# FFN-down: a seven-product square at every second visit in three of the four sweeps

## The chip, the cores and the metric

The kernel runs on one core of one Trainium2 chip. The metric is the device time of one execution in microseconds. Three runs of the kernel before took 1183.07, 1184.19 and 1185.29 us; the median, 1184.19 us, is its time. The engines are named as in the profile: PE multiplies matrices (PEld loads its stationary operand), DVE and ACT work on vectors, POOL is the general engine, and SP issues nearly all loads.

## The reference

One layer of a decoder trunk over 256 tokens with a residual stream of 2048 columns, in float32. After a mixer (pooling and RWKV-7 heads), it computes

```python
h2 = rms_norm(x, mlp_norm[i])
x = x + jnp.square(jax.nn.relu(h2 @ w_ffn_up[i])) @ w_ffn_down[i]
gate = jax.nn.sigmoid(rms_norm(x, ple_norm[i]) @ w_ple_gate[i])
x = x + gate * (p[i] @ w_ple_proj[i])
return rms_norm(x, final_norm)
```

The second line is the FFN: up from 2048 to 8192 columns (FFN-up), a squared ReLU, and down from 8192 to 2048 (FFN-down). The change is in FFN-down.

## The kernel before

**Precision.** Every float32 operand is split into a high half, a copy rounded by ACT to the matmul's format, and a low half, the difference, which DVE computes. A product of two matrices is three matmuls: high times high, high times low, low times high.

**Stages.** A head, the RWKV and pooling work with its input projections, the output projection, and then two halves of the FFN (`ffn_half`, L1301). Each half has FFN-up, which makes eight activation tiles `y` (128 x 2048, high and low half), and two sweeps of FFN-down (`down_sweep`, L1206), one for each 1024 output columns (`pair` 0 and 1). So FFN-down has four sweeps: first half pair 0, first half pair 1, second half pair 0, second half pair 1. After them come the projection of the per-layer embeddings, the gate and the final norm.

**One sweep.** A sweep has 16 visits, one for each `kp`. A visit takes a square of 2 x 2 blocks of the activation (two blocks of 128 features, two of 128 tokens) and two rows of weights of 1024 columns, `rx` and `ry`, each loaded by one DMA of 512 KB on SP (`load_raw`, L149). An ordinary visit (L1277 to L1282) splits both rows (`halves_of`: two ACT copies of 512 columns and one DVE subtraction of 1024 for each row) and does eight block products, 24 matmuls of 512 columns. A seven-product square (L1257 to L1275) is a Strassen-Winograd step: it forms four sums of weight blocks on DVE (`t1` to `t4`, L1268 to L1271, 512 columns each), splits seven weight blocks (one of 512 columns, `wad` in the profile, and three of 1024) and does seven block products, 21 matmuls. In the profile the weights of visit n are named `d_na` and `d_nb` in an ordinary visit; `d_nb`, `d_nc`, `d_nd` and `wad` in a square. The products gather in eight PSUM banks, of which four (`b1`, `b5`, `b6`, `b7`) belong to the squares alone and are added to the result after the last square (L1283 to L1294); the other four are added at the sweep's end (L1297). After the last square of the fourth sweep the transposition of the normalised stream for the gate begins (`between`, `h3t` in the profile).

**Sums of activations.** A square also needs four sums of its activation blocks, high and low half. `activation_sums` (L1191) makes them during FFN-up, as soon as the tile's square is there, for each `kp` in `SEVEN`. Two sets share one tile, and the tiles are taken from slots 0, 2 and 5 of the activation pool. Both sweeps of the half read them.

**Which visits.** `SEVEN` is (1, 3, 6, 8, 11, 13). The first three sweeps use all six, the fourth uses (1, 3, 6, 11): 22 squares in 64 visits. Pair 0 goes through `kp` in order; pair 1 goes 0, 2, 1, 4, 3, 5, 6, ... 15. A place below is the position in that order, counted from 0.

**Order and buffers.** From the end of the output projection on, a scheduler sets the order of instructions on each engine from the program order and priorities: weight splits have priority 20000, the last additions 30000. Six buffers hold raw weights (three `raw`, three `raw2`). High halves have three buffers, low halves three, both shared by all visits; in a square, `wad`, the four weight sums (slot 1) and the fourth split (`graw`, two buffers) have their own. In the fourth sweep hooks at places 5, 8, 11 and 14 (`keep`, L1167) each load and split one part of the last gate panel; its raw load also takes a `graw` buffer. The loads on SP start in the order in which they are issued.

Of the kernel before, what the change touches and what calls it, by code (L numbers as in the profile page):

```python
# [10 lines left out]
F32R = mybir.dt.float32r  # L11
# [29 lines left out]
def trunk(  # L41
# [107 lines left out]
    def load_raw(src, n, name):  # L149
        own = False  # L150
        if deep:
            deep.append(name)
            own = len(deep) > 5 and len(deep) % 6 < 3
        if own:
            raw = fp.tile([128, 1024], F32, tag="raw2", bufs=3, name=f"raw_{name}")
        else:
            raw = wp.tile([128, 1024], F32, tag="raw", name=f"raw_{name}")
        nc.sync.dma_start(raw[:, 0:n], src)
        return raw
# [11 lines left out]
    def split_sb(h_ap, l_ap, src_ap):  # L171
        nc.scalar.activation(h_ap, src_ap, AF.Copy)
        nc.vector.tensor_tensor(l_ap, src_ap, h_ap.bitcast(F32), op=ALU.subtract)
# [115 lines left out]
    def a8(slot, name, dt=F32):  # L289
        return act.tile([128, 2048], dt, tag=f"a{slot}", name=name)  # L290
# [801 lines left out]
    fp = ctx.enter_context(tc.tile_pool(name="fp", bufs=1))  # L1092
# [92 lines left out]

    SEVEN = (1, 3, 6, 8, 11, 13)
    s_slots = (0, 2, 5)

    def activation_sums(box, kp, r):  # L1191

        i = SEVEN.index(kp)
        if i % 2 == 0:
            box[kp] = box[SEVEN[min(i + 1, len(SEVEN) - 1)]] = a8(s_slots[i // 2], f"S{kp}", F32R)
        st = box[kp][:, i % 2 * 1024 : i % 2 * 1024 + 1024]
        t_ = fp.tile([128, 1024], F32, tag="junk", bufs=1, name=f"s{kp}")
        s1, s2_, s3, s4 = (t_[:, j * 128 : (j + 1) * 128] for j in range(4))
        a11, a21, a12, a22 = (r[:, j * 128 : (j + 1) * 128] for j in range(4))
        nc.vector.tensor_tensor(s1, a21, a22, op=ALU.add)  # L1200
        nc.vector.tensor_tensor(s3, a11, a21, op=ALU.subtract)
        nc.vector.tensor_tensor(s2_, s1, a11, op=ALU.subtract)
        nc.vector.tensor_tensor(s4, a12, s2_, op=ALU.subtract)
        split_sb(st[:, 0:512], st[:, 512:1024], t_[:, 0:512])

    def down_sweep(hf, pair, ys, sboxes, hooks=(), between=None, seven=SEVEN):  # L1206

# [16 lines left out]
        def prod(n, a_, w_):  # L1224
            first, last = left[n] == todo[n], left[n] == 1
            left[n] -= 1
            (ah, al), (wh, wl) = a_, w_
            nc.tensor.matmul(banks[n], ah, wh, start=first, stop=False)  # L1228
            nc.tensor.matmul(banks[n], ah, wl, start=False, stop=False)  # L1229
            nc.tensor.matmul(banks[n], al, wh, start=False, stop=last)  # L1230

        def halves_of(src, name, own=False):

            pool, kw = (fp, dict(bufs=2)) if own else (wp, {})
            wh = pool.tile([128, 1024], F32R, tag="graw" if own else "wh", name=f"wh_{name}", **kw)
            wl = pool.tile([128, 1024], F32R, tag="graw" if own else "wl", name=f"wl_{name}", **kw)
            with tc.high_priority(20000):
                for c in range(2):
                    nc.scalar.activation(wh[:, c * 512 : c * 512 + 512], src[:, c * 512 : c * 512 + 512], AF.Copy)
                nc.vector.tensor_tensor(wl, src, wh.bitcast(F32), op=ALU.subtract)  # L1240
            return [(wh[:, c * 512 : c * 512 + 512], wl[:, c * 512 : c * 512 + 512]) for c in range(2)]
# [5 lines left out]
        def add(tt, c, src):  # L1247
            nc.vector.scalar_tensor_tensor(xs(tt, c), src, s2[:, tt : tt + 1], xs(tt, c), op0=ALU.mult, op1=ALU.add)

        for q, kp in enumerate((0, 2, 1, 4, 3, *range(5, 16)) if pair else range(16)):  # L1250
            if q in hooks:
                hooks[q]()
            y, j = ys[kp // 2], kp % 2 * 512
            a11, a21, a12, a22 = ((y[:, j + i * 128 : j + i * 128 + 128], y[:, 1024 + j + i * 128 : 1152 + j + i * 128]) for i in range(4))
            rx, ry = (load_raw(w_down[pair, hf * 32 + 2 * kp + i], 1024, f"{nm}_{kp}_{i}") for i in range(2))
            if kp in seven:
                i = SEVEN.index(kp)  # L1257
                st = sboxes[kp][:, i % 2 * 1024 : i % 2 * 1024 + 1024]
                s1, s2_, s3, s4 = ((st[:, c * 128 : c * 128 + 128], st[:, 512 + c * 128 : 640 + c * 128]) for c in range(4))
                t_ = a8(1, f"t{nm}_{kp}")  # L1260
                t1, t3, t2, t4 = (t_[:, c * 512 : c * 512 + 512] for c in range(4))
                wa = fp.tile([128, 1024], F32R, tag="wa", name=f"wa{nm}_{kp}")
                w11 = wa[:, 0:512], wa[:, 512:1024]
                with tc.high_priority(20000):
                    split_sb(*w11, rx[:, 0:512])
                w21, w22 = halves_of(ry, f"{nm}_{kp}b")
                with tc.high_priority(20000):
                    nc.vector.tensor_tensor(t1, rx[:, 512:1024], rx[:, 0:512], op=ALU.subtract)  # L1268
                    nc.vector.tensor_tensor(t3, ry[:, 512:1024], rx[:, 512:1024], op=ALU.subtract)
                    nc.vector.tensor_tensor(t2, t3, rx[:, 0:512], op=ALU.add)  # L1270
                    nc.vector.tensor_tensor(t4, ry[:, 0:512], t2, op=ALU.subtract)  # L1271
                w1, w3 = halves_of(t_[:, 0:1024], f"{nm}_{kp}c")
                w2, w4 = halves_of(t_[:, 1024:2048], f"{nm}_{kp}d", True)
                for n, a_, w_ in (("1", a11, w11), ("2", a12, w21), ("3", s4, w22), ("5", s1, w1), ("7", s3, w3), ("6", s2_, w2), ("4", a22, w4)):
                    prod(n, a_, w_)  # L1275
            else:
                w11, w12 = halves_of(rx, f"{nm}_{kp}a")  # L1277
                for n, a_, w_ in (("2", a11, w11), ("4", a21, w11), ("3", a11, w12), ("x", a21, w12)):
                    prod(n, a_, w_)
                w21, w22 = halves_of(ry, f"{nm}_{kp}b")  # L1280
                for n, a_, w_ in (("2", a12, w21), ("4", a22, w21), ("3", a12, w22), ("x", a22, w22)):
                    prod(n, a_, w_)  # L1282
            if kp == seven[-1]:  # L1283
                u = fp.tile([128, 512], F32, tag="r", bufs=2, name=f"u{nm}")
                with tc.high_priority(20000):
                    add(0, 0, b1)
                    nc.scalar.activation(u, b1, AF.Copy)
                    nc.vector.tensor_tensor(u, b6, u, op=ALU.add)
                    add(0, 1, b5)
                    add(1, 1, b5)  # L1290
                    add(0, 1, u)
                    nc.vector.tensor_tensor(u, b7, u, op=ALU.add)
                add(1, 0, u)
                add(1, 1, u)  # L1294
                if between is not None:
                    between()
# [4 lines left out]
    def ffn_half(hf):  # L1301
        sboxes = {}
        ys = []
        for i in range(8):
            f = hf * 8 + i
            y = fp.tile([128, 2048], F32R, tag="y", bufs=8, name=f"y{f}")

            def square(bi, bank):
                r = fp.tile([128, 512], F32, tag="r", bufs=2, name=f"r{f}_{bi}")
                r2 = r.rearrange("p (c t) -> p c t", c=2)  # L1310
                nc.scalar.activation(r2, bank[:, :, T : 2 * T], AF.Copy)
                nc.vector.tensor_tensor(r2, bank[:, :, 0:T], r2, op=ALU.add)
                nc.vector.scalar_tensor_tensor(r, r, 0.0, r, op0=ALU.max, op1=ALU.mult)
                split_sb(y[:, bi * 512 : bi * 512 + 512], y[:, 1024 + bi * 512 : 1024 + bi * 512 + 512], r)
                if 2 * i + bi in SEVEN:
                    activation_sums(sboxes, 2 * i + bi, r)

            gemm_wide(w_up[f], h2, f"u{f}", square)
            ys.append(y)
            if f == 1:  # L1320
                inv_ms()

        if hf == 1:
            h3_part, h3 = transposed("h3")
            h3_box.append(h3)

        down_sweep(hf, 0, ys, sboxes)
        if hf == 0:
            down_sweep(hf, 1, ys, sboxes)
        else:  # L1330
            down_sweep(hf, 1, ys, sboxes, {5: keep, 8: keep, 11: keep, 14: keep}, lambda: [h3_part("ple_norm", n) for n in range(2)], (1, 3, 6, 11))
            for n in range(2, 4):
                h3_part("ple_norm", n)

# [149 lines left out]
```

## Time and profile before

| | |
|---|---|
| median of three runs | 1184.19 us |
| the profiled execution | 1184.84 us |
| its span, first to last instruction | 1183.1 us |
| mean granted TensorE clock | 0.997 |
| FFN-down, first half (two sweeps) | 558.9 to 725.0 us of the span |
| FFN-down, second half | 903.3 to about 1073 us of the span |
| PE, DVE, ACT busy | 1166.3, 857.5, 704.5 us |

A row of the timeline gives the start in us from the span's start, the duration, the engine (with a q for its sequencer, which issues DMAs), the line of the kernel, the operation, what is written and read, shapes and a count; in brackets stands the idle time of the engine before it and what ended it. PE's matmuls overlap in these rows, so their rate is read from start to start. A row of windows gives a stretch, its length, and for each engine the busy time in it. A row of one tile gives the least, median and largest duration in ns.

### The profile page before, as it was taken

What the parts mean: (1) busy time and instruction counts of PE and PEld (TensorE: products, weight loads), DVE (VectorE), ACT (ScalarE), POOL (GpSimd) and SP (SyncE); (2) the same over time, 40 slices, a digit from 0 to 9 for tenths busy, and PEclk for the clock granted to TensorE, in tenths of its full rate; (3) what the DMA queues carried; (4) which work ended last, traced back from release to release, by engine and by line L of the source; (5) the groups of instructions that cost most, each with busy time, mean ns of one, the idle gap of its engine ahead of it and who ended that gap; (6) DMA issues with size and microseconds to landing.
All of it is one profiled execution on the core that took longest, in us unless ns stands there. A gap on an engine that the chain in (4) does not pass through costs nothing.

```text
span 1183.1 us, 17263 instructions
## 1 busy us (share of the span) xinstructions
PE 1166.3 (99%) x6428; PEld 976.6 (83%) x6428; DVE 857.5 (72%) x1156; ACT 704.5 (60%) x1302; POOL 13.6 (1%) x73
## 2 busy tenths in 40 slices
PE   9999999999999999999999999999999999999997
PEld 8787777888887888888888888888888888878886
DVE  7686995964656666667888977666678779788543
ACT  7776848676545465555565654554556555668544
POOL 2100000000000000000000000000000000000000
PEclk9999999999999999999999999999999999999999
DMA  8464443354455555656556665655555556767611
GB/s 290 151 198 148 130 144 122 119 179 157 163 199 177 178 181 194 193 184 209 196 183 209 210 217 178 193 185 193 188 188 205 203 195 207 275 219 252 197 54 71
DMA packets 60756, 216.81 MB, mean 183 GB/s; under 512 B 6784, under 2 KB 7552, under 8 KB 60288
## 3 DMA queue, kind: packets, MB, share of 16 engines
q1 hardware_dynamic: 60240, 215.12, 54.5%
q8 instruction: 50, 0.82, 0.3%
q10 hardware_dynamic: 432, 0.60, 0.1%
q14 instruction: 34, 0.28, 0.1%
HBM read 213.59 MB, written 2.10 MB: 182 GB/s over the span
## 4 chain that ended last, share of the span: by engine, by line
PE 95%; ACT 2%; DVE 1%; DMA 1%; issue 0%; POOL 0%; SPq 0%; ACTq 0%; POOLq 0%
PE u_w L1112 20%; PE u_w L1117 10%; PE d_b L1229 8%; PE d_b L1230 8%; PE d_b L1228 8%; PE gt_b L238 2%; PE gt_b L242 2%; PE gt_b L241 2%; PE d_w L1229 2%; PE d_w L1230 2%; PE d_w L1228 2%; PE zk_b L241 1%; PE zk_b L242 1%; PE o_b L241 1%; PE o_b L242 1%; PE zv_b L238 1%
## 5 line engine op out<-in xcount | busy, mean ns | idle before, releaser
L1112 PE MATMUL u_w<-h,wh_u 128*128 128x512 f32 x1024 | 322.2, 396 | 0.0
L167 ACT ACTIVATE wh_u<-raw_u 128x512 fp32r<-128x512 f32 x256 | 147.6, 624 | 163.1 <-issue 96.1
L168 DVE TENSOR_TENSOR wl_u<-raw_u,wh_u 128x1024 fp32r<-128x1024 f32 x128 | 156.7, 1225 | 110.9 <-ACT wh_u L167 109.0
L1117 PEld LDWEIGHTS u_w<-h,wl_u 128*128 128x128 f32 x1024 | 192.5, 188 | 45.1
L1117 PE MATMUL u_w<-h,wl_u 128*128 128x256 f32 x1024 | 201.5, 278 | 0.0
L1112 PEld LDWEIGHTS u_w<-h,wh_u 128*128 128x128 f32 x1024 | 156.0, 189 | 0.1
L168 DVE TENSOR_TENSOR wl_gt<-raw_gt,wh_gt 128x1024 fp32r<-128x1024 f32 x24 | 29.4, 1224 | 23.2 <-ACT wh_gt L167 23.1
L167 ACT ACTIVATE wh_gt<-raw_gt 128x512 fp32r<-128x512 f32 x48 | 28.0, 639 | 23.1 <-PE gt_b L242 14.4
L241 PE MATMUL gt_b<-wh_gt,h 128*128 128x512 f32 x96 | 37.4, 389 | 0.0
L242 PE MATMUL gt_b<-wh_gt,h 128*128 128x512 f32 x96 | 37.4, 389 | 0.0
L168 DVE TENSOR_TENSOR wl_o<-raw_o,wh_o 128x1024 fp32r<-128x1024 f32 x16 | 19.6, 1223 | 12.9 <-ACT wh_o L167 9.9
L167 ACT ACTIVATE wh_o<-raw_o 128x512 fp32r<-128x512 f32 x32 | 18.4, 623 | 16.2 <-issue 8.4
L167 ACT ACTIVATE wh_zp<-raw_zp 128x512 fp32r<-128x512 f32 x32 | 18.6, 623 | 15.9 <-PE zp_b L242 5.7
L168 DVE TENSOR_TENSOR wl_zk<-raw_zk,wh_zk 128x1024 fp32r<-128x1024 f32 x16 | 19.5, 1222 | 9.4 <-ACT wh_zk L167 9.3
L241 PE MATMUL zv_b<-wh_zv,hTh 128*128 128x512 f32 x64 | 26.0, 407 | 0.0
L241 PE MATMUL zk_b<-wh_zk,hTh 128*128 128x512 f32 x64 | 25.8, 404 | 0.0
L241 PE MATMUL zp_b<-wh_zp,hTh 128*128 128x512 f32 x64 | 25.7, 402 | 0.0
L238 PE MATMUL gt_b<-wl_gt,h 128*128 128x512 f32 x96 | 25.7, 389 | 0.0
L242 PE MATMUL zk_b<-wh_zk,hTl 128*128 128x512 f32 x64 | 25.6, 401 | 0.0
L241 PE MATMUL zr_b<-wh_zr,hTh 128*128 128x512 f32 x64 | 25.5, 398 | 0.0
L168 DVE TENSOR_TENSOR wl_zv<-raw_zv,wh_zv 128x1024 fp32r<-128x1024 f32 x16 | 19.4, 1219 | 8.2 <-ACT wh_zv L167 7.3
L242 PE MATMUL zp_b<-wh_zp,hTl 128*128 128x512 f32 x64 | 25.0, 391 | 0.0
(809 smaller groups left out, 2941.4 us busy)
## 6 DMA issues: line engine op xcount, KB each, us to landing
raw_u<-in_w_ffn_up_dram SPq DMA_DIRECT2D x128, 512.0 KB, 3.5
raw_d<-in_w_ffn_down_dram SPq DMA_DIRECT2D x128, 512.0 KB, 4.3
raw_gt<-in_w_ple_gate_dram SPq DMA_DIRECT2D x24, 512.0 KB, 3.4
raw_zk<-in_w_in_dram SPq DMA_DIRECT2D x16, 512.0 KB, 3.6
raw_zr<-in_w_in_dram SPq DMA_DIRECT2D x16, 512.0 KB, 3.4
raw_zv<-in_w_in_dram SPq DMA_DIRECT2D x16, 512.0 KB, 3.4
raw_zp<-in_w_in_dram SPq DMA_DIRECT2D x16, 512.0 KB, 3.3
raw_o<-in_w_out_dram SPq DMA_DIRECT2D x16, 512.0 KB, 4.1
```

The lines of the kernel that those rows point to most:

```text
L167: nc.scalar.activation(wh[:, a * 512 : (a + 1) * 512], raw[:, a * 512 : (a + 1) * 512], AF.Copy)
L168: nc.vector.tensor_tensor(wl, raw, wh.bitcast(F32), op=ALU.subtract)
L238: nc.tensor.matmul(banks[tt], ah[:, ts_], halves[a][1], start=False, stop=last)
L241: nc.tensor.matmul(banks[tt], ah[:, ts_], halves[a][0], start=i + a == 0, stop=False)
L242: nc.tensor.matmul(banks[tt], al[:, ts_], halves[a][0], start=False, stop=False)
L1112: nc.tensor.matmul(bank[:, ct, :].rearrange("p (s t) -> p s t", s=2), wh[:, cs[ct]], hl, start=k == 0, stop=False, skip_group_check=True,)
L1117: nc.tensor.matmul(bank[:, ct, 0:T], wl[:, cs[ct]], hl[:, 0, :], start=False, stop=k == 15, skip_group_check=True)
L1228: nc.tensor.matmul(banks[n], ah, wh, start=first, stop=False)
L1229: nc.tensor.matmul(banks[n], ah, wl, start=False, stop=False)
L1230: nc.tensor.matmul(banks[n], al, wh, start=False, stop=last)
```

## The change

`SEVEN` gets seven members, all odd: (1, 3, 5, 7, 9, 11, 13). A square stands at every second visit. The first three sweeps use all seven, so each has nine ordinary visits instead of ten. The set of sums for 13 has no partner and gets a tile of its own in another pool (`S`, 1024 columns). In pair 1 of the first half the order becomes 0, 2, 1, 4, 3, 6, 5, 8, 7, 10, 9, 12, 11, 14, 13, 15, which puts the squares at places 2, 4, 6, 8, 10, 12, 14; pair 1 of the second half keeps its order. There the fourth sweep uses (1, 3, 7, 11) instead of (1, 3, 6, 11), since 6 no longer has sums. In all there are 25 squares in 64 visits.

```diff
-    SEVEN = (1, 3, 6, 8, 11, 13)
+    SEVEN = (1, 3, 5, 7, 9, 11, 13)
     s_slots = (0, 2, 5)
...
         if i % 2 == 0:
-            box[kp] = box[SEVEN[min(i + 1, len(SEVEN) - 1)]] = a8(s_slots[i // 2], f"S{kp}", F32R)
+            st = a8(s_slots[i // 2], f"S{kp}", F32R) if i < 6 else fp.tile([128, 1024], F32R, tag="S", name=f"S{kp}")
+            box[kp] = box[SEVEN[min(i + 1, len(SEVEN) - 1)]] = st
...
-        for q, kp in enumerate((0, 2, 1, 4, 3, *range(5, 16)) if pair else range(16)):
+        for q, kp in enumerate(((0, 2, 1, 4, 3, *range(5, 16)) if hf else (0, 2, 1, 4, 3, 6, 5, 8, 7, 10, 9, 12, 11, 14, 13, 15)) if pair else range(16)):
...
-            down_sweep(hf, 1, ys, sboxes, {5: keep, 8: keep, 11: keep, 14: keep}, lambda: [h3_part("ple_norm", n) for n in range(2)], (1, 3, 6, 11))
+            down_sweep(hf, 1, ys, sboxes, {5: keep, 8: keep, 11: keep, 14: keep}, lambda: [h3_part("ple_norm", n) for n in range(2)], (1, 3, 7, 11))
```

## The prediction

> **What bounds the kernel now.** I read the page's busy totals first, then the chain that ended last, then TensorE's timeline inside one sweep, then busy time by windows, and last the single rows around the seams.
>
> ```profile
> span 1183.1 us, 17263 instructions
> PE 1166.3 (99%) x6428; PEld 976.6 (83%) x6428; DVE 857.5 (72%) x1156; ACT 704.5 (60%) x1302; POOL 13.6 (1%) x73
> PE 95%; ACT 2%; DVE 1%; DMA 1%; issue 0%; POOL 0%; SPq 0%; ACTq 0%; POOLq 0%
> ```
>
> PE is 99% busy and carries 95% of the chain that ended last. A busy PE can hide gaps, since matmul ends are modelled, so I look at starts instead: the first matmuls of three visits in a row of the first sweep (visit 3, a seven-product square; visits 4 and 5, ordinary).
>
> ```profile
> 574.55 0.39 PE L1228 MATMUL d_w<-wad,y 128*128 128x512 f32 x1
> ...
> 579.31 0.39 PE L1228 MATMUL d_b<-wh_d_4a,y 128*128 128x512 f32 x1
> ...
> 584.75 0.39 PE L1228 MATMUL d_b<-wh_d_5a,y 128*128 128x512 f32 x1
> ```
>
> A square takes 579.31 - 574.55 = 4.76 us for 7 x 3 = 21 matmuls, 0.2267 us each. An ordinary visit takes 584.75 - 579.31 = 5.44 us for 8 x 3 = 24, again 0.2267 us. The spacing is the same in both kinds, so TensorE runs these visits without a gap and the stage is bound by its matmul count. Whether the other engines can go on feeding it is read from windows one pair of visits long (a square and an ordinary visit, 10.2 us) in the second sweep, which already has four squares at every second place:
>
> ```profile
> core 0: us, PE busy (x) PEld busy (x) DVE busy (x) ACT busy (x) POOL busy (x), PEclk, DMA share, GB/s
> 385.00:539.00 154.00, 154.00 (x886) 134.48 (x885) 101.11 (x126) 83.95 (x151) 0.00 (x0) 1.00 0.58 188
> ...
> 647.40:657.60 10.20, 10.20 (x46) 8.38 (x45) 9.47 (x11) 7.75 (x15) 0.00 (x0) 1.00 0.63 212
> 657.60:667.80 10.20, 10.20 (x46) 8.45 (x45) 9.12 (x11) 6.38 (x13) 0.00 (x0) 1.00 0.53 191
> 667.80:678.00 10.20, 10.20 (x46) 8.45 (x45) 8.96 (x11) 6.38 (x13) 0.00 (x0) 1.00 0.58 206
> 678.00:688.20 10.20, 10.20 (x46) 8.45 (x45) 8.89 (x11) 6.38 (x13) 0.00 (x0) 1.00 0.60 217
> ```
>
> The columns after the stretch are busy us of PE, weight load, DVE, ACT and POOL. DVE is the nearest rival: 8.89 to 9.47 of 10.20 us, falling from pair to pair, while PE stays full and the granted clock is 1.00. ACT has 6.38, DMA a share of 0.53 to 0.63.
>
> **The change part by part.**
>
> *Matmuls removed.* Three sweeps get a seventh square, the fourth keeps four: 3 squares x 3 matmuls = 9 matmuls fewer, 9 x 0.2267 = 2.04 us. All of it lies on the path, as PE has no gap there. That is the whole gain by work.
>
> [...]
>
> *Preparation added in the sweeps.* A square costs DVE three 1024-wide subtractions and five of 512; an ordinary visit two of 1024.
>
> ```profile
> 675.27 1.22 DVE L1240 TENSOR_TENSOR wl_d_7a<-raw_d,wh_d_7a 128x1024 fp32r<-128x1024 f32 x1
> 676.40 0.68 DVE L173 TENSOR_TENSOR wad<-raw_d,wad 128x512 fp32r<-128x512 f32 x1
> 677.01 1.22 DVE L1240 TENSOR_TENSOR wl_d_7b<-raw_d,wh_d_7b 128x1024 fp32r<-128x1024 f32 x1
> ...
> 664.99 1.22 DVE L1240 TENSOR_TENSOR wl_d_5a<-raw_d,wh_d_5a 128x1024 fp32r<-128x1024 f32 x1
> ...
> 668.05 0.39 PE L1229 MATMUL d_b<-wl_d_5a,y 128*128 128x512 f32 x1
> ...
> 678.25 0.39 PE L1229 MATMUL d_b<-wl_d_7a,y 128*128 128x512 f32 x1
> ```
>
> From start to start a 1024 takes 676.40 - 675.27 = 1.13 us and a 512 takes 677.01 - 676.40 = 0.61. A square is 3 x 1.13 + 5 x 0.61 = 6.44 us, an ordinary visit 2.26, a pair 8.70 of 10.2: 85%. So at every second visit DVE still has 1.5 us a pair for its waits. The margin of the low half that PE needs first in the ordinary visit (DVE end to first reading matmul) is 668.05 - 666.21 = 1.84 us behind the second square and 678.25 - 676.49 = 1.76 behind the third: nearly a fixed point. With a loss of 0.08 per pair, three more pairs keep 1.5 us. I cost the added 3 x (6.44 - 2.26) = 12.5 us of DVE at nothing; PE covers it. Without cover it would be up to 12.5 us, which is the outer bound; in the other direction it can give nothing, since PE is full.
>
> *Activation sums added.* One more set in each half of the FFN, 2 in all.
>
> ```profile
> L1200 DVE TENSOR_TENSOR s<-r x12: 291/293/294, 406.6 to 884.7; 128x128 f32<-128x128 f32 x12
> ...
> L172 ACT ACTIVATE S<-s x12: 615/616/617, 409.5 to 887.6; 128x512 fp32r<-128x512 f32 x12
> L173 DVE TENSOR_TENSOR S<-s,S x12: 683/684/685, 410.8 to 888.9; 128x512 fp32r<-128x512 f32 x12
> ```
>
> Each is four operations of 0.29 us and one of 0.68 on DVE, 1.84 us, and 0.62 on ACT. They lie in FFN-up, where DVE was busy for 101.11 of 154 us with PE full (first window above): hidden, 0. Uncovered they would cost 2 x 2.5 = 5 us. The separate buffer of the last sum adds no instruction: 0, unless a wait for it appears; its reader of the first half is done a whole FFN-up earlier.
>
> *Square 13 of the second sweep moves one place later.* Its sums of banks (eight DVE operations at the sweep's end) now have one ordinary visit behind them instead of two before FFN-up starts. SP's loads move with their visit; POOL and ACT issue none here.
>
> ```profile
> 713.87 1.41 DVE L1248 SCALAR_TENSOR_TENSOR x<-d_w,s2sq,x 128x512 f32<-128x512 f32 x2
> ...
> 720.94 1.23 DVE L168 TENSOR_TENSOR wl_u<-raw_u,wh_u 128x1024 fp32r<-128x1024 f32 x1
> 722.09 0.75 DVE L1248 SCALAR_TENSOR_TENSOR x<-ud,s2sq,x 128x512 f32<-128x512 f32 x1
> 723.11 2.79 DVE L1248 SCALAR_TENSOR_TENSOR x<-d_b,s2sq,x 128x512 f32<-128x512 f32 x4 [0.28 <-PE d_b L1230]
> 725.82 2.35 DVE L168 TENSOR_TENSOR wl_u<-raw_u,wh_u 128x1024 fp32r<-128x1024 f32 x2
> ...
> 724.95 0.62 PE L1112 MATMUL u_w<-h,wh_u 128*128 128x512 f32 x2
> 727.72 0.63 PE L1112 MATMUL u_w<-h,wh_u 128*128 128x512 f32 x2
> ```
>
> The work from the start of the sums: eight operations at 0.61 to 0.70 = 5.4 us, four last additions 2.7, and the splits of three FFN-up weights 3 x 1.13 = 3.4: 11.5 us. PE wants the third low half after one ordinary visit (5.44), two weights (2 x (727.72 - 724.95) = 5.54) and about 0.45 within the third, 11.4 us, from a point 0.2 us later: 11.6. Copy waits of DVE may add 0.5. Estimate 0 to 0.6 us; I take 0.3, the middle, since the two sums differ by less than one operation.
>
> *The fourth sweep has squares at 1, 3, 7, 11 instead of 1, 3, 6, 11.* The count stays. The first gate load (hook at place 5) now has a visit more before the next square, the second (hook at 8) stands directly behind square 7.
>
> ```profile
> 1012.06 0.33 SPq L1170 DMA_DIRECT2D graw<-in_w_ple_gate_dram  x1
> ...
> 1018.64 1.23 DVE L1175 TENSOR_TENSOR gk<-graw,gk 128x1024 fp32r<-128x1024 f32 x1 [1.16 <-ACT gk L1174]
> 1019.90 1.23 DVE L1240 TENSOR_TENSOR wl_d_6d<-td,wh_d_6d 128x1024 fp32r<-128x1024 f32 x1
> ...
> 1021.18 0.51 PE L1229 MATMUL d_w<-wl_d_6d,S 128*128 128x512 f32 x1
> 1021.52 0.40 PE L1230 MATMUL d_w<-wh_d_6d,S 128*128 128x512 f32 x1
> ...
> SPq L1170 <- PE d_b L1230: 1.2, 1, 1.2
> ...
> raw_d<-in_w_ffn_down_dram SPq DMA_DIRECT2D x25, 512.0 KB, 4.1
> ...
> 1060.22 1.09 PE L1134 MATMUL h3t<-ident,x 128*128 128x128 f32 x8 [1.01 <-DVE h L1141]
> ```
>
> At square 6, PE shows a spacing of 1021.52 - 1021.18 = 0.34, 0.11 over the usual, because the fourth low half ended at 1021.13, behind the gate's. With a visit more that goes: -0.11. The gate load is held for a square's end (SP waited 1.2 us for PE at place 5, where it stands just as directly behind square 3, and PE shows no gap there); SP holds the next raw loads behind it. I take 0, as at place 5; the bounds are 0 and, if the loads of the very next visit were behind it, 4.1 (landing) + 1.2 (copy) + 1.2 (subtraction) = 6.5 us.
>
> *Sum*: -2.04 + 0 + 0 + 0.3 - 0.11 + 0 = -1.85 us. The profiled execution took 1184.84 us (span 1183.1 and 1.74 around it), which would give 1182.99; it stood 0.65 above the median of 1184.19, so against the median the forecast is **1182.3 us**, 0.16% less. About 0.2%, 2.4 us, is what a measurement of this kernel can tell from no change; the runs shown spread over 1183.07 to 1185.29.
>
> **The rivals.**
>
> *The second gate load blocks SP (slower).* Behind square 7 it waits until PE ends that square, and visit 8's raw loads stand behind it in the queue. Price 6.5 us once: 1182.3 + 6.5 = 1188.8. For it: the row of SP waiting for PE. Against: six raw buffers let the loads run up to three visits ahead, and nothing was late behind the first gate load. It decides from 4.2 us of stall.
>
> *DVE falls behind at every second visit (slower).* Seven in a row never occur now. A subtraction that waits for its copy holds everything behind it, and the order on DVE is drawn up anew:
>
> ```profile
> 682.19 1.23 DVE L1240 TENSOR_TENSOR wl_d_8c<-td,wh_d_8c 128x1024 fp32r<-128x1024 f32 x1 [1.09 <-ACT wh_d_8c L1239]
> 683.45 0.69 DVE L1268 TENSOR_TENSOR td<-raw_d 128x512 f32<-128x512 f32 x1
> ```
>
> The 1.09 us wait stood ahead of work whose input had long landed. [...] With one such wait more, a pair takes 8.70 + 2 x 1.09 = 10.9, 0.7 over; the eight pairs that the three sweeps gain (3, 2 and 3) give 5.6 us: 1187.9. Against: the busy share falls over four pairs and the margin nearly holds.
>
> *More comes back than the nine matmuls (faster).* The 1.01 us that PE waits for the h3 transposition goes with the new order around square 11: 1182.3 - 1.0 = 1181.3. For it: that DVE and ACT work there shifts with the gate loads. Against: square 11, its sums and the transposition stay where they are.
>
> *The gain is eaten at the seams.* Between the first and second sweep of each half DVE is dense, and it arrives there after seven squares instead of six.
>
> ```profile
> 626.20:647.00 20.80, 20.80 (x93) 17.23 (x92) 18.44 (x23) 9.74 (x17) 0.00 (x0) 1.00 0.54 161
> ```
>
> DVE has 2.4 of 20.8 us to spare. Arriving late by one or two subtractions (1.1 to 2.3 us a seam, of which PE sees what exceeds DVE's lead, a quarter to half) at two seams gives 0.5 to 2 us: 1182.8 to 1184.3, still within 0.2%. Against: the square before this seam already stands two visits behind another one.
>
> **How the numbers follow.** Forecast as described 0.50, of which 0.10 reads as faster by over 0.2% through the spread of the runs (half of the spread, 1.1 us, exceeds the 0.5 that is missing); more than the matmuls 0.17; seams 0.10; SP blocked 0.10; DVE behind 0.13. So faster 0.27, within 0.2% 0.50, slower 0.23. The likeliest one's own range is 1181.2 to 1183.4. The range runs from 1180.7 (the faster rival less half a microsecond of spread) to 1187.2 (the slower ones as far as about 0.85 of the smaller price); beyond it I leave 0.05 below and 0.13 above.
>
> **What would show it.** Right: 6419 matmuls on PE instead of 6428; starts still 0.227 apart through seven squares in a row; pairs of 10.2 us with DVE near 8.9; no row of PE waiting for a low half in sweeps one to three; square 7 without the 0.34 spacing. Wrong: gaps of PE behind subtractions from the fourth pair on (DVE behind), a gap of several us at visits 8 or 9 of the last sweep with SP waiting for PE (SP blocked), or a gap at the first FFN-up weights of the second half (the moved sums).

## The result, and the profile after

The changed kernel took 1180.08 us (median of six runs, 1179.47 to 1181.17), the kernel before 1184.01 us in the same comparison (1183.07 to 1185.29): a ratio of 0.997 with a 95% interval of 0.9961 to 0.998. It is 3.9 us or 0.3% faster. The forecast was 1182.3 us, 1.9 us faster, with a range that ended at 1180.7. Two later comparisons of the same two kernels, with more executions each, gave 0.998 (0.9971 to 0.9989) and 0.9981 (0.9973 to 0.999), that is 2.3 and 2.1 us by their medians. So most of the question is what the other 1.9 us of the first comparison were.

The page of the changed kernel begins:

```profile
span 1177.7 us, 17287 instructions
PE 1162.0 (99%) x6419; PEld 973.2 (83%) x6419; DVE 872.0 (74%) x1184; ACT 710.5 (60%) x1313; POOL 13.9 (1%) x73
PE 94%; ACT 2%; DVE 2%; DMA 1%; SPq 0%; issue 0%; DVEq 0%; ACTq 0%
```

PE has 6428 - 6419 = 9 matmuls fewer, and is as full as it was. The windows of the changed kernel's second sweep, again one pair of visits each (columns after the stretch: busy us of PE, weight load, DVE, ACT, POOL; then the granted clock, DMA's share and GB/s):

```profile
660.30:670.50 10.20, 10.20 (x47) 8.45 (x46) 8.96 (x11) 6.38 (x11) 0.00 (x0) 1.00 0.60 217
670.50:680.70 10.20, 10.20 (x47) 8.45 (x46) 8.96 (x11) 6.39 (x11) 0.00 (x0) 1.00 0.57 200
680.70:690.90 10.20, 10.20 (x47) 8.45 (x46) 8.96 (x11) 6.39 (x11) 0.00 (x0) 1.00 0.61 214
690.90:701.10 10.20, 10.20 (x47) 8.45 (x46) 8.96 (x11) 6.39 (x11) 0.00 (x0) 1.00 0.56 202
701.10:711.30 10.20, 10.20 (x47) 8.45 (x46) 8.95 (x11) 6.38 (x11) 0.00 (x0) 1.00 0.57 205
```

Five pairs in a row are the same to a hundredth: DVE repeats itself at 8.96 of 10.20 us, and PE has no gap.

Where the profiled executions differ is read from the first matmul of each stage. The first sweep, for one, starts here in the kernel before and in the changed one:

```profile
558.88 0.40 PE L1228 MATMUL d_b<-wh_d_0a,y 128*128 128x512 f32 x1
```

```profile
556.90 0.40 PE L1229 MATMUL d_b<-wh_d_0a,y 128*128 128x512 f32 x1
```

The changed kernel is already 1.98 us ahead at this point, where its TensorE has run the same instructions in the same order. The lengths of all stages, in us, each from first matmul to first matmul; "again" and "third" are further profiles of the same kernels:

| stage | before | before, again | after | after, again | after, third |
|---|---|---|---|---|---|
| start to FFN-up | 379.68 | 377.54 | 377.69 | 378.65 | 377.71 |
| FFN-up, first half | 179.20 | 179.20 | 179.21 | 179.22 | 179.21 |
| first sweep | 82.99 | 82.97 | 82.29 | 82.29 | 82.29 |
| second sweep, FFN-up, second half | 261.41 | 261.32 | 260.72 | 260.68 | 260.64 |
| third sweep | 82.97 | 82.97 | 82.29 | 82.29 | 82.29 |
| fourth sweep | 88.10 | 86.97 | 86.80 | 87.07 | 87.37 |
| embeddings, gate, norm | 108.75 | 108.75 | 108.75 | 108.76 | 108.75 |

The first and the third sweep are 0.68 to 0.70 us shorter in every profile, and the row that holds the second sweep is shorter by 0.60 to 0.77. In the first pair of profiles the three give 0.70 + 0.69 + 0.68 = 2.07 us; the forecast's first term is 2.04. The first pair of profiles differs by 5.3 us; the other 3.3 lie in the start (1.99) and in the fourth sweep (1.30), and both of these vary about as much between two profiles of one kernel (2.14 and 1.13 for before).

*The start.* Windows of 5 to 12 us, before and after:

```profile
5.00:12.00 7.00, 6.02 (x22) 4.79 (x23) 4.79 (x9) 4.62 (x10) 2.87 (x11) 0.76 1.02 370
```

```profile
5.00:12.00 7.00, 5.77 (x32) 4.78 (x32) 4.38 (x9) 4.86 (x10) 3.21 (x11) 1.00 1.03 397
```

The third number from the end is TensorE's granted clock: 0.76 in the first, 1.00 in the second, and the first has 22 matmuls where the second has 32. A narrower window of before has the fall itself, at half the clock; in 4.30 to 7.60 and in 11.10 to 14.00 us the same view shows 1.00:

```profile
7.70:11.00 3.30, 3.30 (x11) 2.83 (x11) 2.21 (x5) 2.76 (x6) 0.54 (x1) 0.50 0.97 364
```

In the timeline of before, two matmuls of 512 columns in this stretch start 0.42 us apart, almost twice the 0.23 of the sweeps:

```profile
9.47 0.63 PE L241 MATMUL zk_b<-wh_zk,hTh 128*128 128x512 f32 x1
9.89 0.63 PE L242 MATMUL zk_b<-wh_zk,hTl 128*128 128x512 f32 x1
```

Of 14 profiled executions of all kernels here, one had this fall at 5 to 12 us and three another at 37 to 42 us; those four spent 379.7 to 380.4 us up to FFN-up, the other ten 377.5 to 378.7. Half the clock for the 3.3 us of this window costs an estimated 1.65 us of matmul time. The times on record go with it: of 111 later executions of the kernel before, the eight with a mean clock of 0.996 took 1184.4 us in the mean, the 37 with 0.997 1183.6, and the 66 with 0.998 or 0.999 1182.7. That is a part of the spread and not all of it, since those with 0.998 alone run from 1181.37 to 1185.08. What brings the fall on is not shown.

*The fourth sweep.* The wait at the transposition of h3, 1.01 us in the first profile of before, is nearly gone (0.01) in the second profile of the same kernel. In the changed kernel it is absent in two profiles and 0.34 in the third. Rows of ACT and PE, before (first), before (again), after (third):

```profile
1056.84 0.63 ACT L1174 ACTIVATE gk<-graw 128x512 fp32r<-128x512 f32 x1 [1.04 <-DMA graw<-in_w_ple_gate_dram]
```

```profile
1053.47 0.62 ACT L1174 ACTIVATE gk<-graw 128x512 fp32r<-128x512 f32 x1
...
1056.84 1.09 PE L1134 MATMUL h3t<-ident,x 128*128 128x128 f32 x8
```

```profile
1050.60 1.16 ACT L1174 ACTIVATE gk<-graw 128x512 fp32r<-128x512 f32 x2 [1.19 <-DMA graw<-in_w_ple_gate_dram]
...
1055.38 1.10 PE L1134 MATMUL h3t<-ident,x 128*128 128x128 f32 x8 [0.34 <-DVE h L1141]
```

In the first profile ACT stood 1.04 us before the copy of a gate part whose load had not landed, and the copies of h3, which PE waits for through DVE, stood behind it. That load took 7.03 us from issue to landing in the first profile and 5.88 in the second. In the third profile of the changed kernel it took 6.26, and ACT did not stand before its copy; there it was the gate load issued just ahead of it, which took 5.46 us instead of 4.96, and ACT stood 1.19 us before that copy where it had stood 0.69 in the first profile. The order on ACT at this place is the same in both kernels.

### The profile page after: what moved, and what is told of

It is laid out like the page before. It is cut to its first block, busy times and chain, and to the rows that moved or that the text cites. A ratio compares the mean times of both kernels' runs of the same rounds, so it can differ in the third digit from the quotient of the medians.

```text
span 1177.7 us, 17287 instructions
## 1 busy us (share of the span) xinstructions
PE 1162.0 (99%) x6419; PEld 973.2 (83%) x6419; DVE 872.0 (74%) x1184; ACT 710.5 (60%) x1313; POOL 13.9 (1%) x73
## 4 chain that ended last, share of the span: by engine, by line
PE 94%; ACT 2%; DVE 2%; DMA 1%; SPq 0%; issue 0%; DVEq 0%; ACTq 0%
PE u_w L1112 20%; PE u_w L1117 10%; PE d_b L1230 7%; PE d_b L1231 7%; PE d_b L1229 7%; PE d_w L1230 2%; PE d_w L1231 2%; PE d_w L1229 2%; PE gt_b L242 2%; PE gt_b L241 2%; PE gt_b L238 2%; PE o_b L241 1%; PE o_b L242 1%; PE zv_b L238 1%; PE o_b L238 1%; PE zp_b L238 1%
## 5 line engine op out<-in xcount | busy, mean ns | idle before, releaser
L167 ACT ACTIVATE wh_zk<-raw_zk 128x512 fp32r<-128x512 f32 x32 | 18.4, 623 | 11.0 <-PE zv_b L242 4.0
```

Of the source, the lines that this page charges most:

```text
L167: nc.scalar.activation(wh[:, a * 512 : (a + 1) * 512], raw[:, a * 512 : (a + 1) * 512], AF.Copy)
```

## The experiments

**The kernel before, a second time** (no edit).

> The kernel before, unchanged, profiled a second time, to see which of its gaps belong to the kernel and which to one execution. Theory A (the gap is the kernel's): TensorE waits again about 1.0 us at the transposition of h3 in the fourth sweep and shows a spacing of about 0.34 us at square 6, and the fourth sweep is 1.3 us longer than its matmul count. Theory B (one execution's accident): those two are absent or of another size, since they hang on when a gate load lands (7.0 us in the first profile). Both expect the slow clock of 5 to 12 us (0.76) to come and go by chance, worth up to 1.6 us. Ratio to the kernel before 1.000, within 0.001.

1182.78 us against 1183.38 for the comparison's own runs of before, ratio 0.9994 (0.9985 to 1.0003). The profile is the second column of the table. Theory B: the long wait, the wide spacing at square 6 and the slow clock at the start are all absent here, so none of them comes with every execution.

**The changed kernel, again and a third time** (no edit).

> The changed kernel, unchanged, profiled a second time. Both theories: the three sweeps shorter by 0.68 us each. Theory A: again no wait of TensorE at the transposition of h3, time 3.3 to 3.9 us below before. Theory B: the wait may appear here too; the mean gain over many executions is then 2.0 us from matmuls plus what the waits differ on average, 2.0 to 3.9.

> The changed kernel once more, timed over many executions. If only its nine matmuls count: 2.0 us faster than before, ratio 0.9983, and a third profile with sweeps of 82.29 us. If the first comparison's 3.9 us were the kernel's own: ratio 0.997 or less.

1181.09 and 1180.74 us, with the two ratios given above. The nine matmuls are worth 0.9983, inside both intervals, and just outside that of the first comparison. These runs don't show why the first comparison drew higher times of the one and lower ones of the other kernel; the profiles show two places where single executions differ, the start by up to 2.8 us (all kernels) and the fourth sweep by 1.1 (before) to 1.3 us (first pair). Chance alone is a thin answer: 48 of 111 later times of the kernel before reach 1183.07, the lowest of the first six, and by that share all six would reach it in under one comparison of a hundred. A difference between chips isn't excluded either. The later comparisons ran on three chips, with medians of before from 1182.58 to 1183.38; the chip of the first isn't on record.

**The places alone.** Six squares in three sweeps as before, two of them at other visits (7 and 9 instead of 6 and 8), and the fourth sweep's third square at place 7.

```diff
-    SEVEN = (1, 3, 6, 8, 11, 13)
+    SEVEN = (1, 3, 7, 9, 11, 13)
...
-(1, 3, 6, 11))
+(1, 3, 7, 11))
```

> No matmul is removed: the kernel before with squares at 1, 3, 7, 9, 11, 13 in three sweeps (six, as before) and 1, 3, 7, 11 in the fourth. Theory A (moving the fourth sweep's third square from place 6 to 7 frees the waits there): 1.1 to 1.3 us faster than before, and no 1.0 us wait at the transposition. Theory B (the wait is an accident of landing): 0 to 0.3 us faster, from the 0.1 to 0.2 at square 6 alone.

1183.51 us, ratio 1.0002 (0.9993 to 1.0011). No gain: the 1.1 to 1.3 us of theory A lie outside the interval, a gain of up to 0.8 us doesn't. The fourth sweep was all the same 87.26 us long in this profile, 0.84 less than in the first of before: one profile of each would have misled here.

**Each half of the FFN alone.**

```diff
+    SEVENS = ((1, 3, 5, 7, 9, 11, 13), (1, 3, 6, 8, 11, 13))
...
     def ffn_half(hf):
+        SEVEN[:] = SEVENS[hf]
...
-(1, 3, 7, 11))
+(1, 3, 6, 11))
```

For the second half alone the two lists are exchanged, the second sweep has its old order, and the fourth has 1, 3, 7, 11.

> The change in the first half of the FFN alone: seven squares in its two sweeps with the new order in the second, the second half as before (six, and 1, 3, 6, 11). Two squares more, so 6 matmuls and 1.36 us. Theory A: 1.4 us faster than before and the wait at the transposition of h3 still there. Theory B: 1.4 us faster as well, the wait there or not by chance. A gain of 2.5 or more would say that the first half gives something beside its matmuls.

> The change in the second half of the FFN alone: seven squares in its first sweep, squares at 1, 3, 7, 11 in the fourth; the first half as before. One square more: 3 matmuls, 0.68 us. Theory B (the fourth sweep's waits are accidents of landing, only matmuls count): third sweep 82.29 us instead of 82.97, fourth sweep 86.8 to 88.1 as in all profiles so far, 0.7 us faster than before, within 1. Theory A (the fourth sweep itself got better by its move to 7): 1.8 to 2.0 us faster.

First half alone: 1181.91 us against 1183.38, ratio 0.9992 (0.9983 to 1.0001). Second half alone: 1182.22 against 1182.77, ratio 0.9995 (0.9987 to 1.0004). Neither interval alone is clear of no change; the differences of the medians, 1.47 and 0.55 us, stand beside 1.36 and 0.68 by matmul count and add to 2.0. In the profiles the first and the third sweep are 82.29 us where they are changed and 82.97 where they aren't. The second half alone is theory B; for the first half both theories expected the same time.

**The copy of one gate part (the fifth, whose load took 7.03 us) moved behind the copies of h3**, in the kernel before.

```diff
+            if kp == 4:
+                es.enter_context(tc.issue_after(seen['h3', 7].ins))
             for a in range(2):
                 nc.scalar.activation(wh[:, a * 512 : (a + 1) * 512], raw[:, a * 512 : (a + 1) * 512], AF.Copy)
```

> The kernel before, with the ACT copy of the fifth gate part put behind the copies of h3 that stand in the fourth sweep, so that a late landing of that load can't hold them. Theory: the wait of TensorE at the transposition of h3 (1.01 us in the first profile, 0 in the second) can't come any more, whatever the load takes; the fourth sweep is 86.8 to 87.3 us. In the mean of many executions 0 to 0.5 us faster than before. Rival (the wait is DVE's, which is dense there, and not the copy's): the wait appears as often as before.

1183.96 us against 1182.77, ratio 1.0008 (0.9999 to 1.0016): no gain, a tendency to a loss. The wait did not go, and a second one came later:

```profile
1058.43 0.63 ACT L172 ACTIVATE ph<-raw_pT 128x512 fp32r<-128x512 f32 x1 [0.66 <-DMA raw_pT<-in_pT_dram]
...
1060.00 0.44 PE L1136 MATMUL h3t<-ident,x 128*128 128x128 f32 x2 [0.42 <-DVE h L1143]
...
1081.93 0.44 PE L1136 MATMUL h3t<-ident,x 128*128 128x128 f32 x2 [1.43 <-DVE h L1143]
```

Now it was the copy of the embeddings, for whose load ACT stood 0.66 us ahead of the same h3 copies. So the expectation that only the gate load could hold them fell. Ahead of the second wait ACT had stood 2.36 us for another gate load. What stands is the form: in this stretch ACT has copies of just issued loads ahead of the h3 copies, and in these profiles the one that landed late was passed on to PE (ACT stood 1.04, 1.19 and 0.66 us, PE then 1.01, 0.34 and 0.42). The rival, that DVE itself is too dense, isn't excluded by this run. Its profile is of its slowest execution (1186.77 us), with a fall of the clock at 37 to 42 us in it.

**How much cover DVE has.** The changed kernel with one weight sum computed two, or four, times more than needed in each square.

```diff
                     nc.vector.tensor_tensor(t3, ry[:, 512:1024], rx[:, 512:1024], op=ALU.subtract)
+                    nc.vector.tensor_tensor(t3, ry[:, 512:1024], rx[:, 512:1024], op=ALU.subtract)
+                    nc.vector.tensor_tensor(t3, ry[:, 512:1024], rx[:, 512:1024], op=ALU.subtract)
```

> The changed kernel with one of the four weight sums computed three times in every square: two more DVE operations of 512, 1.2 us a pair. Theory cover (a pair of visits needs 8.70 us of DVE and has 10.2, and its copy waits shrink when DVE is later): 9.9 of 10.2, within 1 us of the changed kernel. Rival (the waits for copies, 1.1 us a pair, can't be filled): 11.0 of 10.2, 0.8 over in some 20 pairs, 16 us slower.

> The changed kernel with that sum computed five times in every square: four more DVE operations of 512, 2.4 us a pair. Theory cover: 11.1 of 10.2 us, so 0.9 over in some 18 to 20 pairs of the three full sweeps, 15 to 20 us slower than the changed kernel; DVE near 100% there and TensorE waiting for subtractions. Rival (waits can't be filled): 12.2 of 10.2, 35 to 40 us slower. If it is within 2 us, DVE's spare time was read wrongly.

With two more: 1184.57 us, some 3.5 to 3.8 above the changed kernel's later medians; ratio to before 1.0014 (1.0005 to 1.0022). With four more: 1207.72 us, 27 above it; ratio 1.0204 (1.0191 to 1.0218). Both missed the cover theory's price (within 1 us, and 15 to 20) on the slow side, and both stayed well below the rival's (16, and 35 to 40). Windows of two more, a pair in the first sweep and a pair in the second:

```profile
585.00:595.20 10.20, 10.20 (x47) 8.45 (x46) 10.10 (x13) 6.34 (x12) 0.00 (x0) 1.00 0.61 204
```

```profile
673.50:684.00 10.50, 10.44 (x46) 8.31 (x45) 10.16 (x13) 6.24 (x12) 0.00 (x0) 1.00 0.59 200
...
687.47 0.39 PE L1229 MATMUL d_w<-wh_d_7d,S 128*128 128x512 f32 x1
687.92 0.50 PE L1230 MATMUL d_w<-wl_d_7d,S 128*128 128x512 f32 x1
688.25 0.40 PE L1231 MATMUL d_w<-wh_d_7d,S 128*128 128x512 f32 x1
```

In the first and third sweep DVE runs at 10.10 of 10.20 us and PE still has no gap (82.31 and 82.29 us): the waits for copies were filled, as the cover theory says. In the second sweep the order on DVE came out another way: the split of the next ordinary visit, which waited 0.31 us for its copy, stands ahead of the fourth split. The fourth low half of six squares is late: spacings of 0.45 and 0.33 instead of 0.23 twice, a third of a microsecond, six times. That is 2.1 of the 2.5 us by which this sweep is longer than in the changed kernel. With four more a pair takes 11.6 us:

```profile
605.10:616.70 11.60, 11.17 (x46) 8.31 (x46) 11.46 (x15) 6.18 (x11) 0.00 (x0) 1.00 0.58 184
```

DVE is now the bound, 11.46 of 11.60. Four operations at 0.61 taken off leave 9.0 us, the 8.96 of the windows and not the 8.70 that was summed from single rows: the spare time is 1.2 us a pair, not 1.5.

**More squares in the fourth sweep**, as the cover suggests: five (1, 3, 5, 7, 9) or six (with 11), in the order of the second sweep.

```diff
-(((0, 2, 1, 4, 3, *range(5, 16)) if hf else (0, 2, 1, 4, 3, 6, 5, 8, 7, 10, 9, 12, 11, 14, 13, 15)) if pair else range(16))
+((0, 2, 1, 4, 3, 6, 5, 8, 7, 10, 9, 12, 11, 14, 13, 15) if pair else range(16))
...
-(1, 3, 7, 11))
+(1, 3, 5, 7, 9))
```

> The changed kernel with five squares in the fourth sweep too (1, 3, 5, 7, 9) at places 2, 4, 6, 8, 10, in the order that the second sweep has. One square more: -0.68 us against the changed kernel, -2.7 against before. Theory cover: DVE has room for it, since three gate splits of 1.13 us fall into ten visits; ratio 0.9977. Rival (gate loads wait for the fourth split's two buffers, which each square holds): a square's fourth split comes late, 0.1 to 2 us of waits in the fourth sweep, gain eaten.

> The same with six squares (1, 3, 5, 7, 9, 11) at places 2 to 12: -1.36 us against the changed kernel, -3.4 against before by matmul count. Theory cover: DVE needs 8.70 a pair plus up to 1.13 for a gate split, 9.8 of 10.2, barely enough, and its bank sums start one visit later; ratio 0.997 to 0.998. Rival (buffers and the dense end): 1 to 4 us of waits at the gate splits and the transposition, ratio 0.998 to 1.001, slower than with five.

1181.84 and 1182.85 us beside 1180.74 for the changed kernel in the same comparison; ratios to before 0.9997 (0.9988 to 1.0006) and 0.9998 (0.9989 to 1.0006). The rival held in size: the gain is eaten. With five:

```profile
1027.53 1.23 DVE L1175 TENSOR_TENSOR gk<-graw,gk 128x1024 fp32r<-128x1024 f32 x1 [0.34 <-ACT gk L1174]
1028.67 1.22 DVE L1241 TENSOR_TENSOR wl_d_10a<-raw_d,wh_d_10a 128x1024 fp32r<-128x1024 f32 x1
1029.81 1.22 DVE L1241 TENSOR_TENSOR wl_d_7d<-td,wh_d_7d 128x1024 fp32r<-128x1024 f32 x1
...
1031.08 0.50 PE L1230 MATMUL d_w<-wl_d_7d,S 128*128 128x512 f32 x1 [0.39 <-DVE wl_d_7d L1241]
...
1052.99 0.44 PE L1134 MATMUL h3t<-ident,x 128*128 128x128 f32 x2 [1.14 <-DVE h L1141]
```

The fourth split of square 7 stands on DVE behind the subtraction of a gate part and that of the next visit and ends at 1031.03, after PE wants it; the transposition waits 1.14 us, and ACT had stood 0.99 us for a gate load ahead of it. So these rows show the order on DVE and a landing; that the fourth split's two buffers, which it shares with the gate loads, delay anything is not shown. The sweep takes 88.12 us against 86.80 to 87.37: what three matmuls save is lost to two waits. With six, PE waits 0.38 and 0.62 us for the fourth splits of squares 7 and 11 and 0.73 at the transposition, and the sweep takes 87.82 us. The changed kernel remains the fastest of these.

**Filling the gap ahead of a fall of the clock.** The three falls at 37 to 42 us came behind a wait of TensorE for ACT (1.34 and 1.46 us) or POOL (1.17 us). Windows of the kernel with five squares, and its timeline just before:

```profile
37.00:42.00 5.00, 3.99 (x14) 3.28 (x15) 3.42 (x11) 3.21 (x6) 3.48 (x12) 0.66 0.35 110
...
38.01 0.41 PE L464 MATMUL wagT<-ident,wagS 128*128 128x128 f32 x2 [1.46 <-ACT wagS L459]
```

```diff
     head_norm()
     fill(0.00)
+    ready(3)
     wag_out()
```

> The changed kernel with three idle-time matmuls (ones times ones, about 0.2 us each at full clock, into a bank that is not read again) ahead of the transposition of the head's gates, where TensorE waits 0.9 to 1.5 us. Theory (the granted clock falls to 0.66 in 37 to 42 us in some executions, after the longer of these waits, and that is a large part of the spread of single times): the profile shows 1.00 in 37 to 42 us, the spread of the times shrinks, the median is up to 0.7 us lower than the changed kernel's. Rival (the fall has another cause, or the fillers delay the transposition): same or up to 0.6 us slower, spread unchanged.

1180.32 us against 1182.58, ratio 0.998 (0.997 to 0.999): no different from the changed kernel without the fillers. The spread of the nine times, 3.15 us, isn't smaller than the 3.08 of the changed kernel's eleven in its last comparison, and one of the nine (1182.74 us) has a mean clock of 0.996. The clock was 1.00 in that window of this profile, but it was that in 11 of the 14 profiles in all, so this settles nothing.

## Why the prediction was right or wrong

- *Matmuls removed, 2.04 us.* Right: 9 fewer, and 0.68 us in the first and the third sweep (82.97 to 82.29), where every changed profile agrees: 227 ns for each of the three matmuls that such a sweep has fewer.
- *Preparation hidden by PE.* Right. The busy time of a pair was mis-sized, 8.70 by single rows against 8.96 in the windows. The margin's loss of 0.08 a pair did not go on: it is 1.85 us in each of five pairs.
- *Activation sums.* Right: FFN-up of the first half is 179.2 us with and without.
- *Square 13 moved, 0.3 us.* Measured 0. Part of the last additions were put behind the splits of FFN-up, so the second and third low half (x2 below) were ready at 722.36 + 2.35 = 724.71, and PE first read the third at 727.60. Rows of the changed kernel:

```profile
722.36 2.35 DVE L168 TENSOR_TENSOR wl_u<-raw_u,wh_u 128x1024 fp32r<-128x1024 f32 x2
...
726.70 0.75 DVE L1249 SCALAR_TENSOR_TENSOR x<-d_b,s2sq,x 128x512 f32<-128x512 f32 x1
...
727.60 0.40 PE L1117 MATMUL u_w<-h,wl_u 128*128 128x256 f32 x2
```

- *Square 6 moved, -0.11 us.* Sized from one profile, and the size changes from one to the next. Of the four profiles with a third square at visit 6 in the fourth sweep, three show a wider spacing there, with 0.1 to 0.4 us lost; it is missing in the second profile of before. At visit 7 it comes in one of six profiles with four squares there and no added sums, the second of the changed kernel, with 0.34 us lost. So the sign may be right; no run sizes it.

```profile
1021.89 0.39 PE L1229 MATMUL d_w<-wh_d_7c,S 128*128 128x512 f32 x1
1022.34 0.50 PE L1230 MATMUL d_w<-wl_d_7c,S 128*128 128x512 f32 x1
```

- *The second gate load behind square 7.* Right at 0: no gap at visits 8 and 9 in any of the three profiles. Neither slower rival came. The 1.09 us wait shown for the second of them stood ahead of a sum whose load landed only at 682.94, after that wait; what the rival took from it is in the same sweep of before at 697.83, where a subtraction had waited 1.51 us for its copy and the sum behind it started at 699.09 on a load that had landed at 694.72.
- *The faster rival, that the 1.01 us at the transposition goes.* In the first pair of profiles it looks confirmed, with 1.30 us in the fourth sweep. The repeated profiles take it back: 86.97 for before stands inside 86.80 to 87.37 for after.
- *What failed* is the range's low end, "the faster rival less half a microsecond of spread". The measured 1180.08 lies 0.6 us below it. The sum for the likeliest case held: 1.85 us forecast, 2.3 and 2.1 measured in the two larger comparisons, with the 0.3 of square 13 at 0. What was mis-sized is the spread, taken from three times of 1183.07 to 1185.29 and counted with half a microsecond. Later times of the same kernel run from 1181.37 to 1185.65. Their medians by comparison, 1182.58 to 1183.38, lie 0.8 to 1.6 us below the 1184.19 from which the forecast started, and from them the same sum gives 1180.7 to 1181.5, where the changed kernel later measured 1180.74 and 1181.09. With the low end fell the reading that the 1.9 us forecast would mostly be measured as within 0.2%.
- *What stays open* is why this one comparison came out at 3.9 us. Its first pair of profiles shows where such a difference can come from: the profile of before held two chance delays at once, the slow clock at 5 to 12 us and the gate load of 7.03 us. The profile page's clock row doesn't show the first, since it has a 9 (90% or more) in each of its slices of 30 us; a window of 7 us has the 0.76. By the table the two are worth 1.0 to 2.1 us at the start and 0.7 to 1.3 in the fourth sweep. Whether the other executions of that comparison had them isn't shown. That a part of the 3.9 us was luck is likely; how much isn't known.

## What to carry to other kernels

Where PE is full, count matmuls and trust the count: in two sweeps it came out to a hundredth, while what was read from one gap in one profile was gone, moved or of another size in the next. Before a wait is credited to a kernel, profile the kernel a second time, and look at the granted clock in short windows at the start. Cover is best read from windows over a whole period (8.96 us), not from the sum of single rows (8.70), and what it can bear depends on the order: 10.10 of 10.20 was free in two sweeps and not in a third.

## What the runs showed of the hardware that was not expected

TensorE's granted clock fell to a mean of 0.66 to 0.69 in 37 to 42 us in three of 14 executions. There TensorE had just waited 1.17, 1.34 and 1.46 us; behind waits of 1.00 us and less at the same place it stayed at 1.00, and behind another of 1.17 too. The fall at 7.7 us in the first profile of before came behind a wait of 0.88 us; in the first profile of the changed kernel the same matmul had waited 0.91 us, and in the second there were waits of 0.94 and 0.90 that ended at 6.6 and 8.6 us, with the clock at 1.00 in 5 to 12 us of both. So the length of one wait doesn't decide it. The row of the kernel with two more sums (37.00 to 42.00, clock 0.69) is one of the three:

```profile
37.77 0.41 PE L464 MATMUL wagT<-ident,wagS 128*128 128x128 f32 x2 [1.17 <-POOL wband L131]
```

The gate load of 512 KB that held ACT in the first profile, issued at the same place in the same order, took from 5.58 to 7.03 us to land in the five profiles of the two kernels.
